# Keeping both parts of the split input weights in DRAM, and loading them in the later token blocks

## The chip, the cores and the metric

The kernel runs on one core of a Trainium2 chip. The metric is the device time of one execution in microseconds (us). Three runs of the kernel before the change took 805.04, 805.10 and 805.83 us; the median is 805.1 us. A core has five engines that run side by side, each working through its own list of instructions in order: TensorE (PE, matrix products; PEld are its weight loads), VectorE (DVE), ScalarE (ACT), GpSimd (POOL) and SyncE (SP), which here only issues DMA transfers between DRAM and the on-chip memory.

## The reference

One post-norm layer of a hybrid streaming encoder over 2048 frames of a new stream and 8 running streams of 16 frames. One input projection feeds three branches, every branch is multiplied by its own gate, and one output projection with a residual and a LayerNorm closes the layer:

```
h = einsum('btd,de->bte', x, w_in)                 # 1024 -> 2816, float32
a, g_a, u, v, g_b, c1, c2, g_c = split(h)
y_a = pool_mixer(...)                              # trailing means over 2, 4, 8, 16, then 64x64 products
y_b = u * spatial_mix(layer_norm(v), w_s, b_s)     # lower-triangular 128x128 over a chunk, 4 heads
y_c = conformer_tail(c1 * sigmoid(c2), ...)        # causal depthwise conv of 31 taps, LayerNorm, 384x384
mixed = concat(silu(g_a) * y_a, silu(g_b) * y_b, silu(g_c) * y_c)
x_new = layer_norm(ALPHA * x + mixed @ w_out + b_out)
```

The last rows of the pooling and convolution inputs and the normalised v of the running streams are outputs too.

## The kernel before

The tokens are 17 tiles of 128 (tile 16 holds the running streams), in three blocks of 6, 6 and 5 tiles. Each block runs the whole input projection for its tokens, as eight groups of weight columns in the order of `GROUPS`: (c2, c1, c2), (c1, c2, c1), (ga, a), (ga, a), v, gb, u, gc. The branches' own work runs beside the later groups. After the third block comes the output stage: 17 tiles of the output projection with w_out, residual and LayerNorm, and beside its first tiles the rest of branch C for block 2.

Every float32 product is made of one-pass products. An operand is split into a high and a low part, src = hi + lo, and `mm3` adds hi x hi, hi x lo and lo x hi (lines 189 to 191), leaving out lo x lo. A split is one cast on ScalarE (line 152, tile `whi` for weights, `xhi` for tokens, `mhi` for the mixed branches) and one subtraction on VectorE (`wlo`, `xlo`, `mlo`; all of VectorE's planned operations have line 131, that of the wrapper which counts its time). Weights are loaded in pieces of two k-tiles, 128 x 768 (groups of three column tiles) or 128 x 512 (groups of two), 32 pieces for the whole of w_in. A piece goes into one of four places of the `stage` (line 171), and is split into one of six places of the weight ring. In every one of the three blocks all 32 pieces are loaded and split anew, so are the block's eight token rows (`XRow`, line 220).

The order of every engine is written out by a planner: `Clock.pe` counts TensorE's time as products are given, `after(us, fn)` puts a step a while later, and `Clock.dve` counts VectorE's. The 31 taps of each depthwise convolution (tile `acc`) wait in the list `fill`, and `poll` gives VectorE one of them whenever its account lies behind TensorE's. What is left of them is put out where their result is needed, or in later free time, the third block's in the first microseconds of the output stage. `Loader` starts loads as stage places come free, and `hook` makes the splits at given k-steps of a group's last product.

All DMA goes through SP's one queue in program order. An issue that must wait (for a free place, for the data that it stores, or for the transfer eight issues before it on the same semaphore) holds up all issues behind it.

Three places matter below. In the v phase of a block, VectorE makes the low parts `vlo` of the normalised v in turn with taps and splits, and TensorE's spatial mix (`ps_z`, line 672) waits for each. At the start of the output stage GpSimd scales b_out (line 926) and adds it to the first three residual tiles (line 947, tile `xr`); VectorE's first sums `xr<-xr,ps_o` wait for that, and behind those sums stand in VectorE's order the statistics `ost`, the split `mlo` of the fifth tile, and `csqs`, the sums of squares of branch C; ScalarE's `crs` comes at the end of that chain. TensorE waits for all three (`ps_o`, `ps_var`, `ps_rstd`). And early in block 0 SP loads `pool_w`, whose split stands in ScalarE's and VectorE's order among the work of the second group.

Of the kernel before, what the change touches and what calls it, by code (L numbers as in the profile page):

```python
# [9 lines left out]
F32 = mybir.dt.float32  # L10
F32R = mybir.dt.float32r
# [4 lines left out]
P = 128  # L16
KT = D // P
# [8 lines left out]
# Column tiles of 128 of the input projection.  # L26
# [11 lines left out]
# Token tiles of 128 of each block; tile 16 holds the eight running streams.  # L38
BLOCKS = [list(range(0, 6)), list(range(6, 12)), list(range(12, 17))]
TMAX = 768  # L40
# Slots of the weight ring (pieces of two k-tiles), and of the stage for loads.
RING, STAGE = 6, 4
# The output tile by which the last block's convolution is to be done.
TAILQ = 9
# When the first product starts (us), roughly; products before it that keep the clock up.
START = 6.0
WARM = 8
# Between two steps of a block's tail (us of TensorE's time).
STEP = 3.9

# Columns of the packed per-partition constants.
# [9 lines left out]
def splits(total):  # L61
    """Pieces of a block's tokens, whole tiles, at most 3 tiles each."""
    tiles = total // P
    n = -(-tiles // 3)
    out, t = [], 0
    for i in range(n):
        w = -(-(tiles - t) // (n - i))
        out.append((t * P, w * P))
        t += w
    return out  # L70
# [3 lines left out]
def encoder_kernel(ctx: ExitStack, tc: tile.TileContext, a):  # L74
# [9 lines left out]
    # Every engine runs in the order given here.  # L84
    ctx.enter_context(tc.manual_schedule())

    class Clock:
        """TensorE's time as the products are given (us), and the vector engine's; what is to follow
        later waits in `events`, and the convolution's steps in `fill` for the vector engine's free time."""
# [14 lines left out]
    def drain(tag=None):  # L104
        """What is left of the convolution that `tag` names, or all of it."""
# [13 lines left out]
    class Vector:  # L119
        """The vector engine, with its time counted."""  # L120
# [27 lines left out]
    ring = {}  # L148

    def split(hi, lo, src, then=None):  # L150
        """src (float32) = hi + lo exactly, both in the tensor engine's one-pass type."""
# [14 lines left out]
    class Piece:  # L166
        """A load into the stage, and later its split into a piece of the weight ring."""
        def __init__(self, key, src, cols):
            self.key, self.n, self.cols = key, src.shape[1], cols
# [3 lines left out]
        def split(self, then=None):  # L173
# [3 lines left out]
            ring.setdefault(self.key, []).append((hi, lo))  # L177

# [4 lines left out]
    def mm3(outs, kdim=KT, hook=None):  # L183
        """outs: (ps, lhs, rhs); the products of both parts but for lo x lo, below float32's last bit."""
# [18 lines left out]
    def w_in(key, g):  # L203
        """The loads of a group's weights, to be made one by one."""
        w = len(GROUPS[g]) * P
        v = a["w_in"][:, gofs[g]:gofs[g] + KT * w].rearrange("p (k c) -> p k c", k=KT)
        return [lambda k0=k0: Piece(key, v[:, k0:k0 + 2, :], w) for k0 in range(0, KT, 2)]
# [4 lines left out]
    class XRow:  # L212
        """A load of one k-tile of a block's tokens, and later its split."""
        def __init__(self, b, k, mid=None):
# [6 lines left out]
            else:  # L221
                # in two parts with another load between
# [15 lines left out]
    # keeps TensorE's clock up until the first products  # L238
# [6 lines left out]
    # the first block's loads, the first two k-tiles' weights one by one  # L245
# [33 lines left out]
    # sums over the partitions, to all of them  # L279
# [3 lines left out]
    # conv weights halved, since its input is kept doubled  # L283
# [24 lines left out]
    def load_pool():  # L308
        # two groups of 64 channels on the diagonal
# [14 lines left out]
    def keep_lower(w):  # L324
        """Spatial weights [s, h, t], kept where s <= t."""
        nc.gpsimd.affine_select(out=w, in_=w, compare_op=ALU.is_ge, fill=0.0, base=0,
                                pattern=[[0, 4], [1, P]], channel_multiplier=-1)

    after(12, load_pool)
# [7 lines left out]
    def store(q, j, src):  # L337
        """Channels of a token tile's mixed branches, from channel tile j on."""
# [8 lines left out]
    # running streams' states  # L347
# [15 lines left out]
    def stats(src, npiece, nm, then):  # L363
        """Of each row: 1/sqrt(var + eps), and -mean times it, given to `then`."""
# [22 lines left out]
    # weights of branch C's pointwise product  # L387
# [706 lines left out]
```

## Time and profile before

| | |
|---|---|
| median of the runs | 805.1 us (805.04 to 805.83) |
| span of the profiled execution | 802.9 us; 2.2 us of the median lie outside it |
| busy | TensorE 778.2 us, VectorE 659.0, ScalarE 255.0, GpSimd 216.7 |
| DMA | 88.34 MB in 50918 packets, 110 GB/s in the mean; SP's queue busy for 33.9% of 16 engines' span |
| written to DRAM | 18.58 MB |
| block 0, 1, 2 | about 4.5 to 206, 206 to 413, 413 to 588 us |
| output stage | about 588 to 803 us |

The page of the profile gives busy times and the chain that ended last. The answer on waits lists what each engine waited for, the answer by groups gives counts and mean durations, the timeline gives single instructions with the idle time before them in brackets and its releaser, and the windows give busy time, granted TensorE clock (1.00 is full), the DMA share and the GB/s of a stretch. In all of them L131 is the line number of the kernel before.

### The profile page before, as it was taken

What the parts mean: (1) busy time and instruction counts of PE and PEld (TensorE: products, weight loads), DVE (VectorE), ACT (ScalarE), POOL (GpSimd) and SP (SyncE); (2) the same over time, 40 slices, a digit from 0 to 9 for tenths busy, and PEclk for the clock granted to TensorE, in tenths of its full rate; (3) what the DMA queues carried; (4) which work ended last, traced back from release to release, by engine and by line L of the source; (5) the groups of instructions that cost most, each with busy time, mean ns of one, the idle gap of its engine ahead of it and who ended that gap; (6) DMA issues with size and microseconds to landing.
All of it is one profiled execution on the core that took longest, in us unless ns stands there. A gap on an engine that the chain in (4) does not pass through costs nothing.

```text
span 802.9 us, 11388 instructions
## 1 busy us (share of the span) xinstructions
PE 778.2 (97%) x4340; PEld 734.9 (92%) x4340; DVE 659.0 (82%) x930; ACT 255.0 (32%) x457; POOL 216.7 (27%) x226
## 2 busy tenths in 40 slices
PE   8999998999999999989999999999999899999995
PEld 6999997999999999989999999999988678888885
DVE  5998989995588999999667888999777897676665
ACT  5313224314432241431354243442351233231210
POOL 1010077300002005731000201742009344232332
PEclk9999999999999999999999999999999999999998
DMA  7513311225501253111461134222575344425321
GB/s 244 162 53 109 100 60 57 64 66 170 165 28 53 73 133 97 60 40 59 136 199 47 54 83 129 83 69 86 159 236 203 124 138 158 158 108 177 121 79 64
DMA packets 50918, 88.34 MB, mean 110 GB/s; under 512 B 13616, under 2 KB 27440, under 8 KB 50864
## 3 DMA queue, kind: packets, MB, share of 16 engines
q1 hardware_dynamic: 50864, 87.62, 33.9%
q8 instruction: 34, 0.56, 0.3%
q14 instruction: 20, 0.16, 0.1%
HBM read 69.02 MB, written 18.58 MB: 109 GB/s over the span
## 4 chain that ended last, share of the span: by engine, by line
PE 70%; DVE 13%; POOL 6%; issue 4%; DMA 4%; ACT 2%; SPq 0%; POOLq 0%; DVEq 0%; ACTq 0%
PE ps_c L189 6%; PE ps_o L189 5%; PE ps_o L191 5%; PE ps_c L190 5%; PE ps_o L190 5%; PE ps_c L191 5%; DVE acc L131 4%; PE ps_u L191 3%; PE ps_u L189 3%; PE ps_u L190 3%; PE ps_gc L191 2%; PE ps_gc L189 2%; PE ps_gc L190 2%; PE ps_ga L190 2%; PE ps_ga L189 2%
## 5 line engine op out<-in xcount | busy, mean ns | idle before, releaser
L131 DVE SCALAR_TENSOR_TENSOR acc<-cext,cw,acc 128x768 f32<-128x768 f32 (+1 forms) x270 | 265.8, 984 | 4.0
L131 DVE TENSOR_TENSOR wlo<-stage,whi 128x768 fp32r<-128x768 f32 (+1 forms) x99 | 90.0, 919 | 15.8 <-ACT whi L152 15.4
L189 PE MATMUL ps_c<-xhi,whi 128*128 128x384 f32 (+1 forms) x288 | 96.1, 334 | 0.6 <-ACT xhi L152 0.6
L190 PE MATMUL ps_c<-xlo,whi 128*128 128x384 f32 (+1 forms) x288 | 94.7, 329 | 0.9 <-DVE xlo L131 0.9
L191 PE MATMUL ps_c<-xhi,wlo 128*128 128x384 f32 (+1 forms) x288 | 94.1, 327 | 0.0
L152 ACT CAST whi<-stage 128x768 fp32r<-128x768 f32 (+1 forms) x99 | 75.4, 773 | 25.3 <-PE ps_c L190 11.8
L191 PE MATMUL ps_o<-woxhi,mlo 128*128 128x512 f32 (+1 forms) x208 | 81.5, 392 | 1.8 <-DVE mlo L131 1.8
L189 PE MATMUL ps_o<-woxhi,mhi 128*128 128x512 f32 (+1 forms) x208 | 81.9, 394 | 0.0
L190 PE MATMUL ps_o<-woxlo,mhi 128*128 128x512 f32 (+1 forms) x208 | 80.7, 388 | 0.0
L440 POOL COPY halo_c<-cext 128x30 f32<-128x30 f32 x9 | 5.1, 567 | 213.4 <-DVE cext L131 213.4
L190 PEld LDWEIGHTS ps_c<-xlo,whi 128*128 128x128 f32 x288 | 54.4, 189 | 2.4 <-DVE xlo L131 2.4
L189 PEld LDWEIGHTS ps_c<-xhi,whi 128*128 128x128 f32 x288 | 54.5, 189 | 1.4 <-ACT xhi L152 1.2
L191 PEld LDWEIGHTS ps_c<-xhi,wlo 128*128 128x128 f32 x288 | 54.3, 189 | 0.0
L385 ACT ACTIVATE xr<-xr,onm,ors 128x1024 f32<-128x1024 f32 x16 | 19.9, 1244 | 106.3 <-POOL onm L381 106.3
L191 PEld LDWEIGHTS ps_o<-woxhi,mlo 128*128 128x128 f32 x208 | 39.4, 189 | 11.0 <-DVE mlo L131 2.2
L189 PE MATMUL ps_gc<-xhi,whi 128*128 128x384 f32 (+1 forms) x144 | 47.3, 328 | 0.0
L191 PE MATMUL ps_gc<-xhi,wlo 128*128 128x384 f32 (+1 forms) x144 | 47.0, 326 | 0.0
L190 PE MATMUL ps_gc<-xlo,whi 128*128 128x384 f32 (+1 forms) x144 | 46.9, 326 | 0.0
L190 PEld LDWEIGHTS ps_o<-woxlo,mhi 128*128 128x128 f32 x208 | 39.4, 190 | 8.1
L189 PE MATMUL ps_gb<-whi,xhi 128*128 128x384 f32 x136 | 46.8, 344 | 0.0
L189 PE MATMUL ps_u<-whi,xhi 128*128 128x384 f32 x136 | 46.6, 343 | 0.0
L189 PEld LDWEIGHTS ps_o<-woxhi,mhi 128*128 128x128 f32 x208 | 39.6, 190 | 7.5
(188 smaller groups left out, 1967.1 us busy)
## 6 DMA issues: line engine op xcount, KB each, us to landing
stage<-in_w_in SPq DMA_DIRECT2D x71, 384.0 KB, 3.6
xr<-in_x_prompt SPq DMA_DIRECT2D x16, 512.0 KB, 4.9
o_y<-xr SPq DMA_DIRECT2D x16, 512.0 KB, 2.9
stage<-mix SPq DMA_DIRECT2D x17, 384.0 KB, 4.0
stage<-in_w_in SPq DMA_DIRECT2D x24, 256.0 KB, 2.7
stage<-in_xT SPq DMA_DIRECT2D x14, 384.0 KB, 3.8
mix<-yt SPq DMA_DIRECT2D x17, 192.0 KB, 1.9
mix<-mixs SPq DMA_DIRECT2D x17, 192.0 KB, 2.1
```

Of the source, the lines that this page charges most:

```text
L131: return fn(*args, **kw)
L152: nc.scalar.copy(hi, src)
L189: nc.tensor.matmul(ps, lh, rh, start=(k == 0), stop=False)
L190: nc.tensor.matmul(ps, lh, rl, start=False, stop=False)
L191: nc.tensor.matmul(ps, ll, rh, start=False, stop=(k == kdim - 1))
L385: nc.scalar.activation(out=out, in_=src, func=AF.Identity, scale=rs, bias=nm_)
L440: nc.gpsimd.tensor_copy(halo_c[:, j, :], ext[:, Tp:Tp + CONVC])
```

## The change

In block 0 each piece is loaded and split as before; 3 us of the planner's time after its split both parts are also stored to DRAM tiles (`put`, 64 stores; the first piece's by `put_first`). In block 1 all eight groups, and in block 2 the first seven, load the two parts in place of loading and splitting (`Kept`, 120 loads in place of 60). The parts of a group with an even number go to ring places, of one with an odd number the first two pieces to the stage (all four places) and the last two to the ring, so that each piece goes to the place of the piece with its number two groups earlier. The last group of block 2 is loaded and split as before, since the stage and ring are then wanted for w_out. Where block 1 or 2 begins, the token rows and the first group's parts are loaded and split at other steps than before.

```diff
     class Piece:
-        def __init__(self, key, src, cols):
-            self.key, self.n, self.cols = key, src.shape[1], cols
+        def __init__(self, key, src, cols, keep=None):
+            self.key, self.n, self.cols, self.keep = key, src.shape[1], cols, keep
...
             ring.setdefault(self.key, []).append((hi, lo))
+            if self.keep is not None:
+                after(3, lambda: put(self.keep, hi, lo, self.cols))
+
+    def put(keep, hi, lo, cols):
+        for x, part in enumerate((hi, lo)):
+            nc.sync.dma_start(out=keep[:, x], in_=part[:, :, :cols].bitcast(F32))
+
+    class Kept:
+        def __init__(self, key, k, keep, cols, staged):
+            if staged:
+                parts = [stage().bitcast(F32R).rearrange("p (k c) -> p k c", k=2) for _ in range(2)]
+            else:
+                parts = [core.tile([P, 2, 384], F32R, tag=x, bufs=RING, name=x) for x in ("whi", "wlo")]
+            for x, part in enumerate(parts):
+                nc.sync.dma_start(out=part[:, :, :cols].bitcast(F32), in_=keep[:, x])
+            ring.setdefault(key, [None] * (KT // 2))[k] = tuple(parts)
...
+        if key[0] == 0:
+            kept[g] = [dram.tile([P, 2, 2, w], F32, name=f"keep{g}_{k0}") for k0 in range(0, KT, 2)]
...
+    def w_kept(b, g):
+        w = len(GROUPS[g]) * P
+        return [lambda k=k: Kept((b, g), k, kept[g][k], w, g % 2 == 1 and k < 2) for k in range(KT // 2)]
...
+    after(5, put_first)
     after(12, load_pool)
...
         for g in range(LASTG):
-            loads = Loader([(fn, 1) for fn in w_in((b, g + 1), g + 1)])
-            after(6, loads.next)
-            after(9, loads.next)
-            group_work(b, g, loads.hook({1: 1, 3: 1}))
-        if b < LASTB:
-            W = [(fn, 1) for fn in w_in((b + 1, 0), 0)]
-            X = [(lambda k=k: XRow(b + 1, k), 1) for k in range(KT)]
-            loads = Loader(W[:2] + X[:1] + W[2:3] + X[1:3] + W[3:] + X[3:])
-            group_work(b, LASTG, loads.hook({1: 1, 2: 1, 3: 2, 4: 2, 5: 2, 6: 2}))
+            if b == 0 or (b, g + 1) == (LASTB, LASTG):
+                loads = Loader([(fn, 1) for fn in w_in((b, g + 1), g + 1)])
+                after(6, loads.next)
+                after(9, loads.next)
+                group_work(b, g, loads.hook({1: 1, 3: 1}))
+            else:
+                for i, fn in enumerate(w_kept(b, g + 1)):
+                    after(10 + i if g % 2 == 0 and i < 2 else 5 + i, fn)
+                group_work(b, g, None)
+        if b == 0:
+            W = w_kept(b + 1, 0)
+            after(5, W[0])
+            after(6, W[1])
+            loads = Loader([(lambda k=k: XRow(b + 1, k), 1) for k in range(KT)])
+
+            def leave(k):
+                if k in (2, 4):
+                    W[1 + k // 2]()
+                if 2 <= k < 7:
+                    loads.next()
+            group_work(b, LASTG, leave)
             loads.next(3)
-            X = None
+        elif b < LASTB:
+            for i, fn in enumerate(w_kept(b + 1, 0)):
+                after(5 + i, fn)
...
+            def leave(k):
+                if k in (2, 4):
+                    load(k - 2, k - 1)
+                if k == 5:
+                    for i in range(2):
+                        rows[i].split(lambda i=i: load(i + 4))
+            group_work(b, LASTG, leave)
+            for i in range(2, 4):
+                rows[i].split(lambda i=i: load(i + 4))
+            for i in range(4, KT):
+                after((2.5, 3.5, 5.5, 6.5)[i - 4], lambda i=i: rows[i].split())
```

The planner then gives VectorE other work in the places of the splits that are gone, so its order changes at many places; TensorE's and GpSimd's orders are the same in both kernels. Three places show it. At the start of the output stage VectorE's order in the kernel before ends the third block's taps (the two forms of `acc`, for the running streams and the others, in turn) ahead of the first residual sums:

```order
L131 SCALAR_TENSOR_TENSOR acc_4441<-cext_4281,cw,acc_4441 128x512
L131 SCALAR_TENSOR_TENSOR acc_4441<-cexts,cw,acc_4441 128x128
L131 SCALAR_TENSOR_TENSOR xr<-xr,ps_o 128x512 x4
L131 BN_STATS ost<-xr 128x6 x2
L131 BN_AGGR omv<-ost 128x2
```

The same place on VectorE in the changed kernel, from the last splits of w_out on:

```order
L131 TENSOR_TENSOR woxlo_5927<-stage,woxhi_5926 128x768 x2
L131 TENSOR_TENSOR wlo<-stage,whi 128x512
L131 SCALAR_TENSOR_TENSOR xr<-xr,ps_o 128x512 x4
L131 BN_STATS ost<-xr 128x6 x2
L131 BN_AGGR omv<-ost 128x2
```

The taps that stood between the last split and the first sum have moved ahead of the output stage's splits. In block 1's v phase, from the fourth to the seventh `vlo`, VectorE's order in the kernel before:

```order
L131 TENSOR_TENSOR vlo<-vn,vhi 128x288
L131 SCALAR_TENSOR_TENSOR acc_2326<-cext_2158,cw,acc_2326 128x768 x5
L131 TENSOR_TENSOR wlo<-stage,whi 128x768
L131 SCALAR_TENSOR_TENSOR acc_2326<-cext_2158,cw,acc_2326 128x768
L131 TENSOR_TENSOR vlo<-vn,vhi 128x288
L131 SCALAR_TENSOR_TENSOR acc_2326<-cext_2158,cw,acc_2326 128x768
L131 TENSOR_TENSOR wlo<-stage,whi 128x768
L131 TENSOR_TENSOR vlo<-vn,vhi 128x288 x2
```

and in the changed kernel:

```order
L131 TENSOR_TENSOR vlo<-vn,vhi 128x288
L131 SCALAR_TENSOR_TENSOR acc_2557<-cext_2409,cw,acc_2557 128x768 x7
L131 TENSOR_TENSOR vlo<-vn,vhi 128x288
L131 SCALAR_TENSOR_TENSOR acc_2557<-cext_2409,cw,acc_2557 128x768
L131 TENSOR_TENSOR vlo<-vn,vhi 128x288
L131 SCALAR_TENSOR_TENSOR acc_2557<-cext_2409,cw,acc_2557 128x768
L131 TENSOR_TENSOR vlo<-vn,vhi 128x288
```

The splits are gone and taps stand in some of their places. On SP, the rows behind the first group's loads in the kernel before:

```order
L272 DMA cst<-in_cst 128x151
L171 DMA stage<-in_w_in 128x768 x4
L315 DMA pw_320<-in_pool_w 64x64 x4
L171 DMA stage<-in_w_in 128x512 x4
L297 DMA vg<-in_gmlp_ln_g 128x384
```

and in the changed kernel, where `keep_2` is the DRAM tile of the piece that begins at k-tile 2:

```order
L172 DMA stage<-in_w_in 128x768 x4
L184 DMA keep_2_92<-whi 128x768
L184 DMA keep_2_92<-wlo 128x768
L184 DMA keep_4_93<-whi 128x768
L184 DMA keep_4_93<-wlo 128x768
L184 DMA keep_6_94<-whi 128x768
L184 DMA keep_6_94<-wlo 128x768
L184 DMA keep_0_91<-whi 128x768
L184 DMA keep_0_91<-wlo 128x768
L184 DMA keep_0_218<-whi 128x768
L184 DMA keep_0_218<-wlo 128x768
L349 DMA pw_338<-in_pool_w 64x64 x4
```

The loads of pool_w have moved behind ten stores, eight of the first group's parts and two of the second's.

More of the change, by code (lines that the diff above doesn't have):

```diff
@@ L206, in w_in, with put_first @@
         v = a["w_in"][:, gofs[g]:gofs[g] + KT * w].rearrange("p (k c) -> p k c", k=KT)
-        return [lambda k0=k0: Piece(key, v[:, k0:k0 + 2, :], w) for k0 in range(0, KT, 2)]
+        if key[0] == 0:
+            kept[g] = [dram.tile([P, 2, 2, w], F32, name=f"keep{g}_{k0}") for k0 in range(0, KT, 2)]
+        keep = kept[g] if key[0] == 0 else [None] * (KT // 2)
+        return [lambda k0=k0: Piece(key, v[:, k0:k0 + 2, :], w, keep[k0 // 2]) for k0 in range(0, KT, 2)]
+    kept = {}
+    def w_kept(b, g):
+        w = len(GROUPS[g]) * P
+        return [lambda k=k: Kept((b, g), k, kept[g][k], w, g % 2 == 1 and k < 2) for k in range(KT // 2)]
+    def put_first():
+        hi, lo = ring[0, 0][0]
+        put(kept[0][0], hi, lo, 384)
     xhi = [None] * (KT // 2)
@@ L852, in encoder_kernel, with load @@
         for g in range(LASTG):
-            loads = Loader([(fn, 1) for fn in w_in((b, g + 1), g + 1)])
-            after(6, loads.next)
-            after(9, loads.next)
-            group_work(b, g, loads.hook({1: 1, 3: 1}))
-        if b < LASTB:
-            W = [(fn, 1) for fn in w_in((b + 1, 0), 0)]
-            X = [(lambda k=k: XRow(b + 1, k), 1) for k in range(KT)]
-            loads = Loader(W[:2] + X[:1] + W[2:3] + X[1:3] + W[3:] + X[3:])
-            group_work(b, LASTG, loads.hook({1: 1, 2: 1, 3: 2, 4: 2, 5: 2, 6: 2}))
-            loads.next(3)
-            X = None
+            if b == 0 or (b, g + 1) == (LASTB, LASTG):
[18 more added lines that the diff above has]
+            group_work(b, LASTG, leave)
+            loads.next(3)
+        elif b < LASTB:
+            for i, fn in enumerate(w_kept(b + 1, 0)):
+                after(5 + i, fn)
+            rows = {}
+            def load(*ks, b=b):
+                for k in ks:
+                    rows[k] = XRow(b + 1, k)
+            def leave(k):
[9 more added lines that the diff above has]
+                after((2.5, 3.5, 5.5, 6.5)[i - 4], lambda i=i: rows[i].split())
     flush()
```

## The prediction

> **What bounds the kernel now.** I read the page first, then the answer by groups with shapes kept apart, then TensorE's waits, and then the timelines of VectorE and GpSimd at the places that the waits name. The page says who is busy, and what the chain that ended last is made of:
>
> ```profile
> PE 778.2 (97%) x4340; PEld 734.9 (92%) x4340; DVE 659.0 (82%) x930; ACT 255.0 (32%) x457; POOL 216.7 (27%) x226
> PE 70%; DVE 13%; POOL 6%; issue 4%; DMA 4%; ACT 2%; SPq 0%; POOLq 0%; DVEq 0%; ACTq 0%
> ```
>
> TensorE is busy 97% of the span of 802.9 us, so whatever the change frees elsewhere can be worth at most what TensorE loses in waits (and in a slow clock, below). The groups give the price of one split:
>
> ```profile
> L131 DVE TENSOR_TENSOR wlo<-stage,whi 128x768 fp32r<-128x768 f32 x71 | 70.9, 1010 | 14.1 <-ACT whi L152 13.7
> L131 DVE TENSOR_TENSOR wlo<-stage,whi 128x512 fp32r<-128x512 f32 x28 | 19.1, 688 | 1.7 <-ACT whi L152 1.7
> L152 ACT CAST whi<-stage 128x768 fp32r<-128x768 f32 x71 | 58.4, 835 | 10.9 <-DMA stage<-in_w_in 3.5 <-PE ps_u L191 2.1 <-PE ps_gb L191 1.9
> ```
>
> Block 1 loses eight groups of four splits and block 2 seven: 44 pieces of 768 columns and 16 of 512. That is 44 x 1.01 + 16 x 0.69 = 55.4 us off VectorE, and at least 44 x 0.835 = 36.7 us off ScalarE. Neither is on the path for most of the span. TensorE's waits say where VectorE is:
>
> ```profile
> PE ps_z L672 <- DVE vlo L131: 6.6, 9, 1.9
> PE ps_var L538 <- DVE csqs L131: 2.1, 1, 2.1
> PE ps_o L191 <- DVE mlo L131: 1.8, 1, 1.8
> PE ps_rstd L561 <- ACT crs L555: 1.5, 1, 1.5
> ```
>
> The columns are the time in total, the times, and the longest. So about 12 us of TensorE's waits could be touched, in two kinds of places: the products of the spatial mix in branch B's v phase (ps_z), and three waits early in the output stage. Only some of them lie behind removed work.
>
> **The output stage, where I expect most of the gain.** VectorE's timeline shows what runs before the first residual sums (each row: start, duration, engine, line, what, and in brackets the idle time before it with its releaser):
>
> ```profile
> 610.71 0.34 DVE L131 SCALAR_TENSOR_TENSOR acc<-cexts,cw,acc 128x128 f32<-128x128 f32 x1
> 614.49 1.28 DVE L131 SCALAR_TENSOR_TENSOR xr<-xr,ps_o 128x512 f32<-128x512 f32 x2 [3.44 <-POOL xr L947]
> 616.87 1.28 DVE L131 SCALAR_TENSOR_TENSOR xr<-xr,ps_o 128x512 f32<-128x512 f32 x2 [1.09 <-POOL xr L947]
> 618.07 1.28 DVE L131 BATCH_NORM_STATS2 ost<-xr 128x6 f32<-128x512 f32 x2
> 632.88 3.32 DVE L131 TENSOR_TENSOR mlo<-stage,mhi 128x768 fp32r<-128x768 f32 x2 [0.31 <-ACT mhi L152]
> 641.37 0.56 DVE L131 TENSOR_TENSOR csqs<-csqs,csq 128x384 f32<-128x384 f32 x1
> ```
>
> VectorE waits for GpSimd there (3.44 and 1.09 us), and from 618 on it runs almost without a gap up to mlo and csqs, the operations that TensorE waits for. GpSimd's own rows, and the nearest row of the same operation beside an idle VectorE, in block 1:
>
> ```profile
> 602.63 9.34 POOL L926 TENSOR_SCALAR b_out<-b_out 128x1024 f32<-128x1024 f32 x1 [55.47 <-DMA b_out<-in_b_out]
> 612.05 7.16 POOL L947 TENSOR_TENSOR xr<-xr,b_out 128x1024 f32<-128x1024 f32 x3
> 299.80 0.80 POOL L358 TENSOR_SCALAR cexts<-cexts 128x720 f32<-128x720 f32 x1
> ```
>
> The scaling of b_out takes 9.34 us while VectorE works through left-over convolution taps; it ends when they end. By the size of the row at 299.80 it would be 0.80 x 1024/720 = 1.1 us. In the order of the changed kernel no tap is left there, VectorE is idle from the last split of w_out (599.7) on. So I take 1.1 to 2.4 us (2.4 is one of the three additions, 7.16/3), and 9.34 as the far end, if it were something other than VectorE that slowed it. Next comes the residual itself, which must have landed:
>
> ```profile
> 596.89 3.77 SPq L943 DMA_DIRECT2D xr<-in_x_prompt  x5
> DMA to landing us min/median/max: 9.4/10.2/11.3
> ```
>
> The first one lands no earlier than 596.9 + 9.4 = 606.3, the second about 1 us later. The additions then end at about 608.7 and 611.1. The products of the first two tiles are done when the third tile's begin:
>
> ```profile
> 610.57 0.39 PE L189 MATMUL ps_o<-woxhi,mhi 128*128 128x512 f32 x1
> ```
>
> That leaves VectorE's first sum at about 611.0, the second pair at 612.3, and the statistics at 613.7 in place of 618.07: 4.4 us earlier, with no row behind them changed in order. mlo moves ahead of TensorE's need (4.4 over 1.8, the first wait is gone), csqs too (1.8 + 2.1 = 3.9, gone), and crs behind them is late by 1.5 - (4.4 - 3.9) = 1.0. Sum: **-4.4 us**. Bounds: nothing if b_out stays at 9.34, and -5.4 if the third wait goes as well.
>
> A stretch at a low clock follows the third wait:
>
> ```profile
> 639.00:642.00 3.00, 0.88 (x5) 0.39 (x3) 2.77 (x7) 1.45 (x3) 0.00 (x0) 1.00 0.82 260
> 652.00:655.00 3.00, 1.47 (x7) 0.73 (x6) 2.97 (x4) 1.35 (x4) 1.62 (x1) 1.00 0.00 0
> 655.00:659.00 4.00, 4.00 (x13) 3.09 (x12) 3.97 (x8) 1.57 (x3) 1.93 (x4) 0.57 0.99 312
> ```
>
> The column third from the end is the granted clock, the first behind the length is TensorE's busy time. 4.0 us at 0.57 cost 1.7 us. TensorE idled longer in 639 to 642 and kept its clock, so the length of one wait doesn't decide it, and in the changed kernel a wait of 1.0 us and the same short transposes stand there. I leave the 1.7 us in; without them it is a case of its own below. [...]
>
> **Block 1's v phase.** VectorE's rows, and TensorE's two last waits:
>
> ```profile
> 336.93 7.17 DVE L131 SCALAR_TENSOR_TENSOR acc<-cext,cw,acc 128x768 f32<-128x768 f32 x5
> 344.02 1.77 DVE L131 TENSOR_TENSOR wlo<-stage,whi 128x768 fp32r<-128x768 f32 x1
> 347.94 0.95 DVE L131 TENSOR_TENSOR wlo<-stage,whi 128x768 fp32r<-128x768 f32 x1
> 347.14 0.40 PE L672 MATMUL ps_z<-vlo,wsthi 128*128 128x288 f32 x1 [1.61 <-DVE vlo L131]
> ...
> 350.12 0.40 PE L672 MATMUL ps_z<-vlo,wsthi 128*128 128x288 f32 x1 [0.76 <-DVE vlo L131]
> ```
>
> The planner gives VectorE a tap whenever its account runs behind TensorE's, so the place of a removed split is filled again: ahead of the fifth vlo stand seven long operations in both orders (five taps, a split, a tap; now seven taps). That wait of 1.61 us stays, shorter by 0.3 if a tap takes 1.43 (7.17/5) in place of 1.77. Ahead of the sixth there is one long operation fewer, 0.95 us, which covers the wait of 0.76. I take **-0.9 us**, between 0 and -2.4. Block 2 and the first waits of this phase keep their counts: 0, at most -0.5. Block 0's share of the 6.6 us isn't touched, since its order on VectorE is the same.
>
> **What the change adds.** 64 stores in block 0 and 120 loads for 60 in the later blocks, all in SP's one queue. SP around the end of the first group, ScalarE's cast of pool_w, VectorE's split of the last two pieces of group 1, and what DMA did:
>
> ```profile
> 17.87 4.47 SPq L171 DMA_DIRECT2D stage<-in_w_in  x4
> 22.39 3.09 SPq L315 DMA_DIRECT2D pw<-in_pool_w  x4
> 32.22 0.40 ACT L152 CAST poolwhi<-pw 128x256 fp32r<-128x256 f32 x1
> 31.31 2.00 DVE L131 TENSOR_TENSOR wlo<-stage,whi 128x768 fp32r<-128x768 f32 x2 [0.27 <-ACT whi L152]
> 0.00:206.00 206.00, 198.87 (x1117) 193.10 (x1118) 174.87 (x207) 67.76 (x116) 48.25 (x63) 0.99 0.36 112
> 0.00:20.00 20.00, 17.35 (x78) 13.72 (x79) 10.51 (x16) 10.17 (x14) 2.33 (x15) 1.00 0.77 245
> 60.00:120.00 60.00, 60.00 (x347) 59.72 (x345) 54.28 (x70) 15.89 (x29) 18.94 (x23) 1.00 0.29 91
> mix<-mixs SPq DMA_DIRECT2D x17, 192.0 KB, 2.1
> ```
>
> Ten stores of 393 KB now stand ahead of pool_w's loads. The first 20 us moved 245 GB/s at a share of 0.77, so 318 GB/s at a full one. Four loads and ten stores from 17.9 on are 5.5 MB, 17.3 us at that rate: pool_w lands at about 36, not before 32.2. ScalarE and VectorE wait some 4 us for it in their order, with the drain of two PSUM groups behind them; six banks cover TensorE, each with 24 products of 60/347 = 0.173 us, and VectorE's delay is made good in 60 to 120, where it idles 60 - 54.3 = 5.7 us. I take **+0.3** (0 to +2). In the later blocks a group's parts are asked for a whole group ahead, and 88 MB becomes 88 + 22.5 + 21 = 131 MB, 164 GB/s over the span, half of 318: 0. Between blocks 1 and 2 the token rows come later:
>
> ```profile
> 411.81 2.05 ACT L494 ACTIVATE sgc<-ps_gc 128x384 f32<-128x384 f32 x4 [1.24 <-PE ps_gc L191]
> 413.76 1.35 ACT L152 CAST xhi<-stage 128x640 fp32r<-128x640 f32 x2
> ```
>
> The third row's cast now stands behind the four gates (413.9), its low part is ready 0.7 + 0.8 us later at 415.4, and block 2 (from 413.2; a k-tile is six products of 384 columns and six of 256, 6 x 0.173 + 6 x 0.115 = 1.73 us) asks for it at 416.7. The seventh has to wait for a stage place until 415.4 and some 3.3 us for its load, and is 2 us early. I take **+0.3** (0 to +3).
>
> The slot of a stored part can be written again only when the store has landed; a store of 192 KB lands in 2.1 us, less than a load. [...]
>
> Sum against the profiled execution: 802.9 - 4.4 - 0.9 + 0.3 + 0.3 = 798.2, and the median of the runs (805.1) lies 2.2 us over this span: **800.4 us**.
>
> **The rivals.**
> *The clock comes back too*: the last wait is too short for the low clock, 800.4 - 1.7 = 798.7 us. For it: the rows at 639, a longer wait without it. Against it: the transposes behind the wait are the same.
> *The gain doesn't arrive*: b_out's scaling is slow by the full DMA queues of those microseconds, not by VectorE, and only block 1's 0.9 us are left: 805.1 - 0.9 + 0.6 = 804.8. Against it: the operation ends 0.9 us behind the last tap.
> *Slower, stores against block 0*: block 0 moves 112 GB/s x 206 us = 23 MB now and 45.6 MB with the stores, 221 GB/s. At 318 GB/s there is room; but if stores mixed with loads run at two thirds of it (212 GB/s), SP's queue is late from the first group on (two of its last pieces take places whose parts are being stored), the block becomes one of DMA, and it takes 45.6/0.212 = 215 us for 206: 800.4 + 9 = 809.4. It decides below 221 GB/s. For it: no window of this trace mixes stores and loads at a high rate. Against it: the loads alone reach 245 at a share of 0.77.
> *More than that*: freed VectorE time also removes block 1's 1.61 us and the third wait: 800.4 - 1.7 - 1.3 - 1.0 = 796.4.
>
> **How the numbers follow.** The forecast 0.40, the clock as well 0.24, the gain that doesn't arrive 0.11, stores against block 0 (or the token rows late by 3 us and more) 0.18, more than that 0.07. The range from 796.4 to 805.5 leaves out most of the slower case and half of the last. A measurement of this kernel can tell 0.2% (1.6 us) from no change: faster is 0.40 + 0.24 + 0.07 + 0.01 = 0.72, within it 0.11 (the gain that doesn't arrive, and a small part of the slower case), slower 0.17.
>
> **What would show it.** Right: b_out's scaling under 2.5 us, the first xr sum at its products' end without a wait for GpSimd, mlo and csqs gone from TensorE's waits, crs left with about 1 us, a vlo of about 1.3 us left in block 1, and VectorE's busy time lower by some 55 us. Wrong: a wait of TensorE on whi or wlo in the first 60 us, on xhi or xlo at the start of a block, or b_out still near 9 us with VectorE idle.

## The result, and the profile after

The changed kernel takes 798.77 us (797.74 to 799.21, 4 runs), the kernel before 805.07 us beside it (804.99 to 805.83, 4 runs): a ratio of 0.9923, with a 95% interval of 0.9907 to 0.9939. The forecast was 800.4 us, so the gain is 6.3 us where 4.7 were expected. The profiled execution, the quickest of the four, has a span of 795.9 us for 802.9.

On the page of the changed kernel, the busy times and the DMA total:

```profile
PE 775.4 (97%) x4340; PEld 733.7 (92%) x4340; DVE 610.3 (77%) x870; ACT 213.6 (27%) x397; POOL 217.8 (27%) x226
DMA packets 74917, 132.90 MB, mean 167 GB/s; under 512 B 15600, under 2 KB 41712, under 8 KB 74864
```

VectorE has 48.7 us less to do (55.4 by the count of splits; most of the difference is that the rows of neighbouring operations overlap by some 0.08 us each, so 60 rows fewer shorten the busy time by less than their sum), ScalarE 41.4 us less, and 133 MB are moved (131 forecast). The same product starts at these times in the two traces (TensorE's order is the same in both, so one start can be set against the other):

| start of | before | after | shift | since the row above |
|---|---|---|---|---|
| block 1 | 206.25 | 205.72 | -0.53 | -0.53 |
| block 2 | 413.17 | 411.85 | -1.32 | -0.79 |
| output stage | 588.60 | 588.27 | -0.33 | +0.99 |
| ps_var behind csqs | 641.99 | 637.73 | -4.26 | -3.93 |
| ps_rstd behind crs | 654.11 | 648.86 | -5.25 | -0.99 |
| next ps_var | 661.27 | 654.43 | -6.84 | -1.59 |

The last column is what the stage that ends at this row gained or lost; the next ps_var is the place where the low clock behind crs has ended. Nearly all of the gain, 6.5 us, comes in the output stage, and 1 us is given back in block 2. TensorE's waits after the change (total, times, longest):

```profile
PE ps_z L707 <- DVE vlo L131: 6.2, 5, 1.8
PE ps_z L707 <- ACT vhi L152: 2.1, 1, 2.1
PE tp_b L741 <- DVE yb L131: 0.7, 2, 0.5
PE ps_rstd L596 <- ACT crs L590: 0.6, 1, 0.6
PE ps_o L208 <- ACT sgc L529: 0.5, 1, 0.5
```

The waits for mlo and csqs are gone, crs is left with 0.6 us, and the sum of the waits for vlo has hardly changed. The wait for vhi, in block 0, has grown; in the kernel before it was

```profile
PE ps_z L672 <- ACT vhi L152: 0.8, 1, 0.8
```

GpSimd's and VectorE's timelines at the start of the output stage:

```profile
600.88 1.05 POOL L993 TENSOR_SCALAR b_out<-b_out 128x1024 f32<-128x1024 f32 x1 [46.22 <-DMA b_out<-in_b_out]
604.71 7.15 POOL L1014 TENSOR_TENSOR xr<-xr,b_out 128x1024 f32<-128x1024 f32 x3 [2.78 <-DMA xr<-in_x_prompt]
...
609.25 2.67 DVE L131 SCALAR_TENSOR_TENSOR xr<-xr,ps_o 128x512 f32<-128x512 f32 x4 [9.68 <-PE ps_o L210]
611.84 1.28 DVE L131 BATCH_NORM_STATS2 ost<-xr 128x6 f32<-128x512 f32 x2
627.62 3.34 DVE L131 TENSOR_TENSOR mlo<-stage,mhi 128x768 fp32r<-128x768 f32 x2 [0.31 <-ACT mhi L152]
636.14 0.56 DVE L131 TENSOR_TENSOR csqs<-csqs,csq 128x384 f32<-128x384 f32 x1
```

VectorE is idle for 9.68 us until TensorE releases its first sum; everything behind it comes 5.2 to 6.2 us earlier than before. The full DMA queues, to which the rival of the gain that doesn't arrive put the 9.34 us of b_out's scaling, are as full here (a share of 1.00, ahead of the last column), and the scaling takes 1.05 us:

```profile
600.00:604.00 4.00, 4.00 (x19) 3.26 (x19) 0.00 (x0) 0.00 (x0) 1.05 (x1) 1.00 1.00 396
```

The windows behind crs show the clock (third column from the end):

```profile
646.00:650.00 4.00, 3.35 (x15) 2.28 (x14) 3.97 (x4) 1.60 (x4) 2.37 (x2) 1.00 0.07 27
650.00:654.00 4.00, 4.00 (x20) 3.25 (x19) 3.96 (x8) 1.57 (x3) 2.18 (x4) 1.00 1.01 313
```

It is 1.00 where the kernel before had 0.57. But it is low at a place where it was full before, in block 0 behind the longer wait for vhi (the kernel before, then the changed one):

```profile
122.00:126.00 4.00, 3.51 (x19) 3.00 (x20) 3.41 (x5) 1.35 (x4) 2.94 (x5) 1.00 0.36 103
122.00:126.00 4.00, 3.62 (x13) 3.62 (x14) 3.91 (x6) 1.36 (x3) 3.31 (x5) 0.58 0.56 197
```

### The profile page after: what moved, and what is told of

It reads as the page before. It is cut to its first block, busy times and chain, and to the rows that moved or that the text cites. A ratio compares the mean times of both kernels' runs of the same rounds, so it can differ in the third digit from the quotient of the medians.

```text
span 795.9 us, 11385 instructions
## 1 busy us (share of the span) xinstructions
PE 775.4 (97%) x4340; PEld 733.7 (92%) x4340; DVE 610.3 (77%) x870; ACT 213.6 (27%) x397; POOL 217.8 (27%) x226
## 4 chain that ended last, share of the span: by engine, by line
PE 63%; DVE 17%; DMA 6%; POOL 6%; issue 4%; ACT 2%; SPq 2%; DVEq 0%; POOLq 0%; ACTq 0%
DVE acc L131 9%; PE ps_o L208 7%; PE ps_o L210 7%; PE ps_o L209 6%; PE ps_c L208 4%; PE ps_c L209 4%; PE ps_c L210 4%; PE ps_u L210 2%; PE ps_u L208 2%; PE ps_u L209 2%; PE ps_gc L210 2%; PE ps_gc L208 2%; PE ps_gc L209 2%; DVE s L131 1%; PE ps_gb L208 1%
## 5 line engine op out<-in xcount | busy, mean ns | idle before, releaser
L208 PE MATMUL ps_c<-xhi,whi 128*128 128x384 f32 (+1 forms) x240 | 80.0, 333 | 0.1
L209 PE MATMUL ps_c<-xlo,whi 128*128 128x384 f32 (+1 forms) x240 | 79.2, 330 | 0.6 <-DVE xlo L131 0.5
L210 PE MATMUL ps_c<-xhi,wlo 128*128 128x384 f32 (+1 forms) x240 | 78.6, 328 | 0.0
L131 DVE TENSOR_TENSOR xlo<-stage,xhi 128x768 fp32r<-128x768 f32 (+2 forms) x26 | 21.5, 853 | 42.4 <-ACT xhi L152 42.4
L724 POOL TENSOR_TENSOR zb<-zb,sgb 128x384 f32<-128x384 f32 x17 | 39.8, 2354 | 30.7 <-ACT sgb L723 23.0
L209 PE MATMUL ps_u<-wlo,xhi 128*128 128x384 f32 x136 | 45.6, 335 | 0.0
L210 PE MATMUL ps_u<-whi,xlo 128*128 128x384 f32 x136 | 45.6, 335 | 0.0
L209 PE MATMUL ps_v<-wlo,xhi 128*128 128x384 f32 x136 | 45.5, 334 | 0.0
L210 PE MATMUL ps_v<-whi,xlo 128*128 128x384 f32 x136 | 45.5, 334 | 0.0
L208 PE MATMUL ps_v<-whi,xhi 128*128 128x384 f32 x136 | 45.5, 334 | 0.0
```

Of the source, the lines that this page charges most:

```text
L131: return fn(*args, **kw)
L208: nc.tensor.matmul(ps, lh, rh, start=(k == 0), stop=False)
L209: nc.tensor.matmul(ps, lh, rl, start=False, stop=False)
L210: nc.tensor.matmul(ps, ll, rh, start=False, stop=(k == kdim - 1))
L724: after(11, lambda i=i, sg=sg: nc.gpsimd.tensor_tensor(out=zb[:, i, :], in0=zb[:, i, :], in1=sg, op=ALU.mult))
```

## The experiments

Three explanations stand against each other: the gain comes from the taps that left the output stage (the theory); it comes from less work on VectorE and ScalarE in general; or from the clock alone. Each kernel was timed beside the kernel before on its own chip, so ratios are compared, not times.

**The taps put back.** The changed kernel, with a floor under the planner's list in the last block:

```diff
-        while fill and Clock.dve < Clock.pe - 0:
+        while fill and Clock.dve < Clock.pe - 0 and len(fill) > ring.get("hold", 0):
...
+        if b == LASTB:
+            ring["hold"] = 21
...
+    ring["hold"] = 0
     both = [out_runs(q) for q in range(2)]
```

> The changed kernel, in which the last 21 taps of the third block's convolution are held back until the first residual sums of the output stage, where they stood before the change; nothing is left out and no split or transfer differs. Theory (the gain of the output stage comes from the taps that left VectorE there): b_out's scaling takes 9 us again, TensorE's waits for mlo (1.8 us), csqs (2.1 us) and crs (1.5 us) return, and the time rises by 4.2 us at least, and by 6.7 us with the low clock, to 803.0 to 805.5 us. Rival (the gain comes from less work on VectorE and ScalarE as a whole, or from the clock alone): within 1.6 us of the changed kernel's 798.8 us.

Measured: 803.72 us (800.31 to 804.78, 10 runs) beside 804.42 us of the kernel before (800.81 to 805.77, 19 runs), a ratio of 0.9992 (0.9976 to 1.0007). So 21 taps, which keep VectorE busy from 598.27 to 608.65, undo the whole gain, while all 60 splits stay removed. In the trace two things differ from what was expected. The wait for mlo did not return, and the one for csqs did so at less than half its length:

```profile
PE ps_rstd L596 <- ACT crs L590: 1.5, 1, 1.5
PE ps_var L573 <- DVE csqs L131: 0.9, 1, 0.9
```

And b_out's scaling took 1.08 us, not 9. GpSimd and VectorE in this kernel:

```profile
605.73 9.93 POOL L1016 TENSOR_TENSOR xr<-xr,b_out 128x1024 f32<-128x1024 f32 x3 [3.68 <-DMA xr<-in_x_prompt]
...
610.95 1.28 DVE L131 SCALAR_TENSOR_TENSOR xr<-xr,ps_o 128x512 f32<-128x512 f32 x2 [2.29 <-PE ps_o L210]
613.33 1.28 DVE L131 SCALAR_TENSOR_TENSOR xr<-xr,ps_o 128x512 f32<-128x512 f32 x2 [1.09 <-POOL xr L1016]
```

Here the first of the three additions was held up (9.93 us for 7.15) until the taps had ended, and the statistics begin at 614.53, 2.7 us later than with the taps gone. This profiled execution took 801.2 us, one of the quicker ones of a kernel that spreads over 4.5 us, so what its slower runs lose on top, 2.5 us at the median, is in no trace. The low clock is back with the wait for crs:

```profile
651.00:655.00 4.00, 4.00 (x12) 3.08 (x13) 3.97 (x9) 1.57 (x4) 1.46 (x4) 0.60 0.90 275
```

**The kernel before, once more.**

> The kernel before, unchanged, for a second profile. Theory (the low-clock stretches depend on where a wait falls and can come or stay away in the same kernel): the two stretches near 141 and 656 us differ in length or place from those of the first profile, by up to 1.7 us each. Rival (they belong to the kernel's waits): both are there again, 1.4 to 1.7 us each. The first 30 us, which hold the same instructions in both kernels, show what their loss (4.1 us before, 3.2 us after) varies by.

It took 805.56 us, and it shows the same place from the other side. GpSimd's rows, and three taps of VectorE:

```profile
600.73 1.11 POOL L926 TENSOR_SCALAR b_out<-b_out 128x1024 f32<-128x1024 f32 x1 [55.10 <-DMA b_out<-in_b_out]
604.58 7.67 POOL L947 TENSOR_TENSOR xr<-xr,b_out 128x1024 f32<-128x1024 f32 x3 [2.75 <-DMA xr<-in_x_prompt]
...
604.67 2.89 DVE L131 SCALAR_TENSOR_TENSOR acc<-cext,cw,acc 128x512 f32<-128x512 f32 x1
607.48 2.49 DVE L131 SCALAR_TENSOR_TENSOR acc<-cexts,cw,acc 128x128 f32<-128x128 f32 x1
609.90 2.90 DVE L131 SCALAR_TENSOR_TENSOR acc<-cext,cw,acc 128x512 f32<-128x512 f32 x1
```

A tap of 0.34 us takes 2.49, one of 0.74 takes 2.9: each waits out one addition of 2.4 us. In the first profile it was GpSimd that stood still for 9.34 us while the taps ran at their usual 0.34 and 0.74. So the two engines exclude each other here, and which of them is held differs between executions of one kernel. The scaling began at 602.63 in one and at 600.73 in the other; what decides was not tried. VectorE's first sum comes at 614.49 in one execution and 616.69 in the other. Of the two stretches at a low clock, the one behind crs is there again and the one near 141 us is not, so each explanation is right about one of them:

```profile
656.00:660.00 4.00, 4.00 (x13) 3.09 (x12) 3.97 (x8) 1.58 (x3) 1.95 (x4) 0.58 1.00 333
...
139.00:142.00 3.00, 3.00 (x19) 3.00 (x20) 3.00 (x5) 1.75 (x5) 1.61 (x1) 1.00 0.69 223
```

Of the first 30 us TensorE is busy for 27.74 here, for 26.97 in the first profile and for 27.87 in the changed kernel's: one kernel varies there by nearly as much as the two kernels differ.

**One block alone.** Two kernels in which only one of the later blocks loads the kept parts (each with the load and split order of the kernel before at the other's edge):

```diff
-            if b == 0 or (b, g + 1) == (LASTB, LASTG):
+            if b != 1 or g + 1 == LASTG:          # block 1 alone
...
+            if b < LASTB or g + 1 == LASTG:       # block 2 alone
```

> Only block 1 loads the kept parts (its groups 0 to 6); block 2 loads and splits all its weights as before the change, and block 0 stores as in the changed kernel. Theory: VectorE's 26 us freed in block 1 end as idle time at its end and the taps of block 2 stay in the output stage, so 803.5 to 805.5 us. Rival (each freed microsecond counts alike): half of the gain, 802 us.

> Only block 2 loads the kept parts (its groups 0 to 6); block 1 loads and splits all its weights as before the change, block 0 stores as in the changed kernel. Theory: the taps leave the output stage, so nearly the whole gain is there: 798 to 800.5 us, with block 1's waits for vlo as before the change (4.2 us in place of 3.4). Rival (each freed microsecond counts alike): 802 us.

Measured: block 1 alone 804.68 us (ratio 1.0009, 0.9988 to 1.0030), block 2 alone 797.86 us (0.9923, 0.9904 to 0.9943). Half of the removed splits give nothing, and the other half everything. TensorE's waits with block 1 alone, and with block 2 alone:

```profile
PE ps_o L210 <- DVE mlo L131: 2.4, 2, 1.8
PE ps_var L573 <- DVE csqs L131: 2.1, 1, 2.1
```

```profile
PE ps_z L707 <- DVE vlo L131: 6.2, 6, 1.9
PE ps_rstd L596 <- ACT crs L590: 0.6, 1, 0.6
```

That rules out the gain by work in general. The clock alone is ruled out by the table above, where 4.9 of the output stage's 6.5 us come ahead of the stretch that was low.

**The changed kernel, once more.**

> The changed kernel, unchanged, on another chip and beside the kernels of this call. Theory (what spreads the times of the kernel before, 800.8 to 805.8 us, is which of GpSimd and VectorE holds the other up at the start of the output stage, and the changed kernel has no taps there): all runs within 1.5 us of each other, near 798.5 us. Rival (the spread comes from the chip's clock or memory): a spread of 4 to 5 us as in the kernel before.

Measured: 798.03 us (797.79 to 798.94, 4 runs), while the kernel before spread from 803.36 to 807.30 us beside it (9 runs). Block 2 alone spread from 797.36 to 798.25. In sets of four runs, the changed kernel and block 2 alone, which have no taps in the output stage, stay within 0.9 to 1.5 us. The kernel before, block 1 alone and the taps put back spread over 2.7 to 5.7 us in sets of 7 to 19 runs, though the four runs of the kernel before beside the first result lay within 0.9 us. This fits a spread that comes from which engine is held, but doesn't show it. The two profiled executions of the kernel before differ by only 1.0 us, and no quick one was profiled. The clock may have a part: of the 19 runs the four under 802 us all had a mean granted clock of 0.998, the highest that occurs; three slower ones had it too.

With two profiles of each kernel, the stages can be compared by their lengths in us (the last one up to the next ps_var of the table above):

| stage | before | before, again | after | after, again |
|---|---|---|---|---|
| block 0 | 206.25 | 204.92 | 205.72 | 206.51 |
| block 1 | 206.92 | 206.66 | 206.13 | 206.12 |
| block 2 | 175.43 | 175.44 | 176.42 | 176.38 |
| output stage | 72.67 | 75.22 | 66.16 | 65.74 |

What the change does in blocks 1 and 2 repeats within 0.3 us. Block 0 varies by 1.3 us in one kernel, and the output stage of the kernel before by 2.5.

**The additions moved to VectorE.** The kernel before, with the three additions taken off GpSimd (which still scales b_out):

```diff
-    for q in range(3):
-        add_bias(q)
     both = [out_runs(q) for q in range(2)]
     mm3([r for t in both for r in t])
+    for q in range(3):
+        nc.vector.tensor_tensor(out=resid[q], in0=resid[q], in1=bc["b_out"], op=ALU.add)
```

> The kernel before, with the first three additions of b_out moved from GpSimd to VectorE, behind the taps and ahead of the residual sums; nothing else differs. Theory (a tap and a GpSimd operation exclude each other, so that the three additions of 2.4 us lie in line with the taps): in place of 7.2 us of GpSimd the line holds 3 x 1.2 us of VectorE, the statistics come 1 to 3 us earlier than at 618 to 619 us, and the time is 801 to 804 us with less spread. Rival (VectorE's own work bounds the place, GpSimd's operations run beside it): 3.7 us more on VectorE make it slower, 807 to 808.5 us.

Measured: 802.17 us (801.39 to 803.94, 6 runs), a ratio of 0.9964 (0.9949 to 0.9978). VectorE's timeline:

```profile
611.26 3.48 DVE L1002 TENSOR_TENSOR xr<-xr,b_out 128x1024 f32<-128x1024 f32 x3
614.67 2.47 DVE L131 SCALAR_TENSOR_TENSOR xr<-xr,ps_o 128x512 f32<-128x512 f32 x4
```

VectorE does 3.5 us more and the kernel is 0.4% faster: the three additions had been in line with the taps, not beside them. This trace also has a wait for crs as long as in the kernel before, and the clock behind it is full; it is low at another place, behind the wait for mlo:

```profile
653.09 0.91 PE L561 MATMUL ps_rstd<-ident,crs 128*128 128x128 f32 x3 [1.53 <-ACT crs L555]
654.00:658.00 4.00, 4.00 (x19) 3.25 (x19) 3.96 (x8) 1.58 (x3) 1.96 (x4) 1.00 1.00 327
636.00:640.00 4.00, 4.00 (x12) 3.17 (x11) 3.84 (x7) 1.32 (x3) 0.00 (x0) 0.57 0.41 135
```

**The stores made twice.** Where would the slower rival begin? Each store of block 0 is followed by a second one, to a DRAM tile that nothing reads:

```diff
             nc.sync.dma_start(out=keep[:, x], in_=part[:, :, :cols].bitcast(F32))
+            again = dram.tile([P, 2, cols], F32, name=f"again{len(twice)}")
+            twice.append(again)
+            nc.sync.dma_start(out=again, in_=part[:, :, :cols].bitcast(F32))
```

> The changed kernel with each of the 64 stores of block 0 made twice, the second to DRAM tiles that nobody reads: block 0 then moves 23 + 45 + 22.5... of that 23 MB as before and 45 MB of stores, 68 MB in 206 us, 330 GB/s. Theory of the slower rival (mixed stores and loads reach no more than 318 GB/s, from a share of 0.77 at 245 GB/s): block 0 becomes one of DMA, at least 8 us longer, 807 us and more, with TensorE waiting for whi or wlo. Rival (380 to 419 GB/s hold for mixed traffic too): no wait for weights in block 0, at most 2 us over the changed kernel, 798 to 801 us.

Measured: 813.83 us (812.81 to 815.06), a ratio of 1.0097 (1.0080 to 1.0114), 15.8 us over the changed kernel timed beside it. Two of its waits:

```profile
PE ps_ga L213 <- ACT whi L152: 8.0, 1, 8.0
PE ps_ga L215 <- DVE wlo L131: 4.5, 2, 3.8
```

and two of its windows (the last column is GB/s, ahead of it the DMA share):

```profile
20.00:40.00 20.00, 19.45 (x111) 19.05 (x110) 12.62 (x15) 6.00 (x10) 0.72 (x2) 1.00 0.97 367
60.00:100.00 40.00, 27.51 (x139) 26.37 (x138) 35.21 (x43) 8.52 (x18) 4.92 (x7) 0.79 0.93 296
```

The mechanism is real: TensorE waits 12.5 us for the third group's weights, whose loads stand behind the stores in SP's queue. It needs twice the stores, though. With mixed traffic the rate at a full share is 367/0.97 = 378 GB/s in the first of these windows and 296/0.93 = 318 in the second, so the prediction's 318 is the low end, and the rival's 380 the high one.

**Block 0's cost, and the waits for vlo.** Five kernels on what the change costs or leaves. First pool_w's loads ahead of the stores:

```diff
-        after(8, lambda: split(*pw, w))
+        after(18, lambda: split(*pw, w))
...
-    after(12, load_pool)
+    after(2, load_pool)
```

> The changed kernel, in which pool_w's four loads are issued ahead of the ten stores that stood before them; its split stays where it was on ScalarE and VectorE. Theory (these stores cost some 0.5 us, by a delay of VectorE in the second group that lasts into block 0's v phase): pool_w's cast no longer waits, VectorE's 2.2 us of idle time before pool_w's low part go, the first wait for vhi near 119 us is 0.5 us shorter, and the time is 797.3 to 798.3 us. Rival (the delay is made good before the v phase and costs nothing): 798.0 to 798.8 us with the wait for vhi as before.

In the changed kernel ScalarE waited for pool_w, and VectorE behind it:

```profile
36.19 0.41 ACT L152 CAST poolwhi<-pw 128x256 fp32r<-128x256 f32 x1 [3.72 <-DMA pw<-in_pool_w]
...
36.63 0.43 DVE L131 TENSOR_TENSOR poolwlo<-pw,poolwhi 128x256 fp32r<-128x256 f32 x1 [2.23 <-ACT poolwhi L152]
```

With the loads first, in the same two places:

```profile
33.00 0.40 ACT L152 CAST poolwhi<-pw 128x256 fp32r<-128x256 f32 x1
...
34.93 0.42 DVE L131 TENSOR_TENSOR poolwlo<-pw,poolwhi 128x256 fp32r<-128x256 f32 x1
```

and of TensorE's waits there is

```profile
PE ps_z L707 <- ACT vhi L152: 1.5, 1, 1.5
```

The wait for vhi is 1.5 us, where the profiles with pool_w's loads behind the stores have 2.1 to 2.8, and the time 797.29 us (ratio 0.9892, 0.9874 to 0.9910). The trace bears the theory out; the times alone don't separate it from the changed kernel (0.9907 in its second measurement, 0.9892 to 0.9922).

Then no taps between the vlo of a run, in blocks 0 and 1:

```diff
-        while fill and Clock.dve < Clock.pe - 0:
+        while fill and Clock.dve < Clock.pe - 0 and not Clock.quiet:
...
+            def quiet(by):
+                Clock.quiet += by
+            if b < LASTB:
+                after(8, lambda: quiet(1))
             for h in range(4):
                 after(8 + 1.5 * h, lambda h=h, mix=mix: mix(h))
+            if b < LASTB:
+                after(13.6, lambda: quiet(-1))
```

> The changed kernel, in which the planner gives VectorE no taps between the first and the last vlo of a run of three tiles in blocks 0 and 1 (the taps come later in the same block). Theory (the waits for vlo come from refilled taps ahead of them, at 1.4 us each beside GpSimd): block 1's two waits (0.95 and 1.88 us) and one of block 0's (0.95 us) shrink or go, 795.5 to 797.5 us. Rival (GpSimd's own chain of small operations and normalisations bounds vlo): the waits for vlo turn into waits for vhi of the same length, 798.5 us.

> The last two edits together, the pause of the taps lasting 1.4 us longer so that it takes in the fourth vlo of each run: no taps between vlo in blocks 0 and 1, and pool_w's loads first. Theory: both add up, and block 1's remaining wait of 1.0 us goes: 794.3 to 795.6 us. Rival: GpSimd's chain bounds what is left, 795.9 us as without the second edit.

> The kernel with both edits, and the pause in block 2 too; so that its taps still end ahead of the output stage, the planner lets VectorE run 4 us ahead of TensorE's account in block 2. Theory (block 2's wait of 1.5 us for the second vlo comes from two taps of 1.1 and 1.6 us beside GpSimd): that wait goes, 793 to 794.5 us. Rival (the earlier taps of block 2 hold up other work of VectorE by as much): no gain over the kernel without the third edit, or a loss.

> The pause of the taps in its first, shorter form (blocks 0 and 1, until 13.6 us) and pool_w's loads first. Theory (both edits are worth what they were worth alone, and the longer pause was what cost): a ratio to the kernel before of 0.986 to 0.988, 0.1% below that of the pause alone (0.9879). Rival (the low clock near 141 us or the chip's start takes the half microsecond back): the ratio of the pause alone, 0.988.

The short pause gave 795.85 us (ratio 0.9879, 0.9864 to 0.9894), as the theory had it: vlo's waits fell from 6.2 us to 4.4.

```profile
PE ps_z L708 <- DVE vlo L132: 4.4, 4, 1.5
PE ps_z L708 <- ACT vhi L153: 2.1, 1, 2.1
```

The longer pause was a miss: 797.22 us (0.9893, 0.9878 to 0.9908). The taps that it holds back come in a block of 20 later, and TensorE waits for yb behind them, 1.8 us for 0.7; vlo's waits came to 5.6 us. The pause in block 2 (for its run of three tiles) missed in the same way, 798.07 us (0.9905, 0.9886 to 0.9924): the wait for the second vlo went, and these came.

```profile
PE tp_b L749 <- DVE yb L133: 2.6, 2, 1.4
PE ps_rstd L598 <- ACT crs L592: 1.7, 2, 1.1
```

The short pause with pool_w's loads first is the fastest kernel of the study: 794.06 us (793.84 to 795.35, 5 runs) beside 805.68 us, a ratio of 0.9865 (0.9845 to 0.9885). Whether it beats the short pause alone the intervals don't tell.

## Why the prediction was right, and where its sizes were off

*The output stage* (-4.4 us forecast, up to the clock). The mechanism held: without taps b_out's scaling takes 1.05 us (1.1 forecast), mlo and csqs are never waited for, crs is left with 0.6 us (1.0 forecast). The size was off by a step on TensorE: the first sums were put at the start of the third tile's products, about 611.0. The four sums of the first two tiles are built side by side, so the first of them is done nine products, 2.1 us, ahead of the last, and VectorE began at 609.25. The residual was early as well: the first addition began at 604.71, where the sum had 606.3. By the table the stage up to crs brought 3.93 + 0.99 = 4.9 us, in spite of 0.5 us of a new wait for sgc at its start, which the second profile of the changed kernel doesn't show.

*The reason given for 9.34 us* was half of the truth. The prediction read it as GpSimd held up by VectorE, from one execution. It goes both ways, and in the one execution seen the other way cost more: 616.69 for the first sum in place of 614.49. Neither matters once the taps are gone, which is why the number came out.

*The clock* (left in by the forecast; a rival at 0.24). At its own place this rival came true, with 1.6 us of its 1.7. The low clock (0.57, 0.58 and 0.60 over 4 us) followed a wait for crs of 1.5 us in both profiles of the kernel before and with the taps put back, but not with the additions on VectorE (1.00), where the wait was the same. It stayed away (1.00) behind one of 0.6 us in both profiles of the changed kernel and with block 2 alone. The prediction's argument, that a longer wait at 639 had kept its clock, did not carry over to this place; what sets the clock was not tried, and stays open.

Over the whole execution the clock did not come back. The first profile of the changed kernel has a low stretch near 124 us (0.50 from 123 to 126), behind a wait for vhi of 2.1 us; the second, where this wait was 2.8 us, has the same mean granted clock (0.995) and ran at 1.00 at the two other places, 139 to 145 and 640 to 660 us. The first profile of the kernel before, where this wait is 0.8, was at 1.00 from 122 to 126. Such a stretch costs some 1.7 us (4 us at 0.58). The first profile of the kernel before has two such stretches (a mean granted clock of 0.993), its second profile and both of the changed kernel by this mean one each (0.995). The stretch near 141 us is another matter: from 139 to 145 us the clock was 0.72 in the first profile of the kernel before, with block 1 alone and with pool_w's loads first, and 1.00 in the second profile of the kernel before, in both of the changed kernel, with the taps put back, with block 2 alone and with the short pause. Its going (1.7 us in block 0, 6 us at 0.72) is chance, not the change. The length of one wait doesn't decide it here: in the first profiles the low stretches stood behind waits of 1.5 us (crs), 1.9 (vlo) and 2.1 (vhi), and the wait for vlo ahead of 141, 1.88 us in the kernel before, is there in the changed kernel too (1.85), with the clock full behind it.

*Block 1* (-0.9): -0.8 measured. The last wait went; the one before it, 1.6 us before the change and 1.3 by the forecast, is 1.7.

*Block 2* (0, at most -0.5): +1.0 measured, in both profiles, so the sign was wrong. Counting long operations between two vlo was the step that failed. Before the change a split of 0.95 us stood ahead of the second vlo; now two taps stand there, 0.96 us in the planner's account, and in the trace

```profile
517.50 1.10 DVE L131 SCALAR_TENSOR_TENSOR acc<-cexts,cw,acc 128x128 f32<-128x128 f32 x1
518.53 1.57 DVE L131 SCALAR_TENSOR_TENSOR acc<-cext,cw,acc 128x512 f32<-128x512 f32 x1
520.03 0.55 DVE L131 BATCH_NORM_STATS2 vst<-ps_v 128x6 f32<-128x384 f32 x1
520.72 0.43 DVE L131 TENSOR_TENSOR vlo<-vn,vhi 128x288 fp32r<-128x288 f32 x1
521.20 0.41 PE L707 MATMUL ps_z<-vlo,wsthi 128*128 128x288 f32 x1 [1.30 <-DVE vlo L131]
```

they take 2.67 us, beside GpSimd's normalisation of v (`vn<-vn,vg`, 1.77 us from 516.69, and `vn<-vn,vb`, 1.02 us from 518.54); two such taps at 514.76 and 515.02 took 0.35 and 0.74. TensorE waits 1.3 us for the second vlo.

*Block 0* (+0.3): pool_w's cast came at 36.19, where the prediction had it at about 36. The delay was not made good in full: VectorE comes 0.5 us late into the v phase, GpSimd's chain with it, TensorE's wait for vhi is longer by 1.3 and 2.0 us than before, and in the first profile the low clock near 124 us (0.58 from 122 to 126) follows it. In the first table that is hidden by two things that are chance: the first 30 us were 0.9 us shorter in this execution, and the low clock near 141 us stayed away. Against the second profile of the kernel before, block 0 is 0.8 and 1.6 us longer. So this term was too small, though within its range. The 2.1 us that the prediction read for a store of 192 KB were low for these stores, without a consequence here: those of 384 KB land in 4.1 us (high parts) and 3.6 us (low parts) in the median.

*The edges of the blocks* (+0.3): no wait for xhi or xlo there, 0. *Stores against block 0* (0.18): not at this size. The rival needed less than 221 GB/s at a full share, and mixed traffic ran at 318 to 378.

*The number.* 800.4 us against 798.8 is closer than the terms are. The clock behind crs (1.6 us) and 0.5 us more from the output stage were missed on one side, 1.0 us in block 2 on the other, and block 0 came out at -0.5 for +0.3 because of what the first profile happened to hold. That these nearly cancel is luck. That the gain came where it was forecast, by the taps that left the output stage, is not.

## What to carry to other kernels

Work taken off an engine that is not the bound pays only where that engine ends a wait, and a planner that refills the freed time decides where that is: here 28 of 60 removed splits gave all of it, because they moved the last taps out of one place. Price an operation by the engine that runs beside it, not by its mean: a tap was 0.34 us or 2.49. And look at a second execution before a reason is read from one long row.

## What was not expected of the hardware

The taps on VectorE (`acc<-cext,cw,acc`) and GpSimd's operations on tiles of 128x1024 (`b_out<-b_out`, `xr<-xr,b_out`) did not slow each other, they excluded each other: 2.49 us for a tap of 0.34 us beside an addition of 2.4 us, or 9.34 us for a scaling of 1.1 us beside taps that took their 0.34 and 0.74. Which of them waited changed between executions of one kernel. The time spread with the taps there and hardly without them, 803.36 to 807.30 us over 9 runs of the kernel before against 797.79 to 798.94 over 4 of the changed kernel on the same chip; that the one comes from the other is argued, not shown.

TensorE's granted clock was halved (0.50 from 123 to 126 us in the changed kernel), for some 1.7 us of loss each time (4 us at 0.57 to 0.60), behind waits as short as 1.5 us, and not behind every such wait: the same wait for crs was followed by a low clock in three profiles (0.57, 0.58 and 0.60) and by a full one in a fourth (1.00).
